# Pairing the scan groups' values in a hybrid decoder trunk on one core

## The chip, the core and the metric

The program runs on one core of a Trainium2 chip. The metric is device microseconds of one execution; the times shown are medians of several runs, and the profile is of one further execution.

## What is computed

The reference is a trunk of two layers over a sequence of 256 tokens of width 1024, float32 throughout. Each layer normalises the stream, multiplies it by one wide input matrix (1024 x 12832), and feeds three token mixers side by side: a Mamba-2 scan, sliding-window attention with sinks, and forgetting attention. Each mixer's output is gated, projected, weighted by a sigmoid gate and summed; the sum goes through one output matrix and is added to the stream. Cut to what the change touches, the scan of one group of four heads (G = 4 groups, chunks of 128 tokens, states of 128):

```python
cb = jnp.einsum('bclgn,bcsgn->bgcls', cc, bc)
y_diag = jnp.einsum('bgrcls,bcsgrp->bclgrp', cb[:, :, None] * decay, x_dt)
...
states = jnp.einsum('bcsgn,bgrcs,bcsgrp->bcgrpn', bc, decay_states, x_dt)
...
y_off = jnp.einsum('bclgn,bcgrpn,bgrcl->bclgrp', cc, prev, jnp.exp(a_cum))
return (y_diag + y_off).reshape(b, s, g, r, p)
```

## The kernel before

**Dense products.** A float32 product is made of three products of rounded halves: hi·hi, lo·hi and hi·lo. The weights come as parts of 512 KB. SyncE loads a part into a `raw` buffer (`load_part`, L363), ScalarE rounds it to `hi` (L293), VectorE subtracts to get `lo` (L294), and then the raw buffer is free. There are N_RAW = 6 raw buffers, 6 each of `hi` and `lo`, and TensorE's program holds at most AHEAD = 4 parts. A load is issued as soon as the part whose buffer it takes has been split; `load_to` (L368 on) asks for it in the order of the stream.

**Units.** Most of TensorE's row is units of 16 dense products (eight of 128x512, eight of 128x256) into one PSUM bank of the tag mm, of which there are three in a ring. The bank is emptied by ScalarE and VectorE: in `chan_sum` (L476 to L482) ScalarE copies one half (L481) and VectorE adds the other (L482); after L482 the bank can be written again, three units later. The other five banks (tag mx) serve everything else.

**What interrupts the units.** Between units the program pumps generators (`pump`, L150) that wait for a time on a model clock, for a token, or for a condition. The scan's is `ssd_group` (L855), one generator per group of heads. It loads the cumulated decays broadcast to all partitions (L861), takes a token "ssd", and then prepares: four transposes of x on TensorE, dt times x on VectorE (L871), the decay differences (L877, L885 eight times), exponentials on ScalarE, the product of dt·x with the decay to the chunk's end (L879). After a pause, one product of C and B (L897, L898) and three multiplications with the decays on VectorE (L901). Then it stands as a `Half`: a step whose products use half of the array and which should be put where other such steps stand. When it goes on, it issues the group's values: 24 matmuls of 64 columns into one mx bank (L907 to L916), and VectorE adds them to D·x (L919, twice). At the end it gives back the token.

The forgetting attention's steps are alike (`fox_quad`, L1058, and `attn_quad`, L586), one generator per quad of heads, four quads a layer: scores (16 matmuls with 64 rows into four mx banks), softmax on VectorE (L649, L658, L661) and ScalarE (L655), transposes, and then values. The values of two quads are kept back in `y.values` and issued ahead of the third quad's scores (L593 to L595); those of the last pair are issued by the last quad itself, and `y.closing` is true when only these are left. A step of TensorE that goes to half-array products and back to dense ones is called an excursion here.

**Around the scan** run the units of the gate z of the scan's branch (`u_z`, L928), whose end (`normed`, L949 to L957) needs the group's values: VectorE multiplies (L951), and splits the result for the projection (L294, L297). `u_conv`, gates (L1102) and projections follow or precede.

**What sets the order.** TensorE's row is as the program writes it. VectorE's, ScalarE's and GpSimd's rows are ordered by a scheduling layer from that program; SyncE issues loads in the stream's order. Each engine goes through its row strictly one after another.

**Tokens before.** T_SSD = 1: one group on chip at a time. Group 0, 1 and 2 go on from `Half` when another half-array step of the second branch stands ready, or at the latest 12 units of the model clock after (D_MEET); group 3 when `y.closing` is true and another stands ready:

```python
limit_ = clock["t"] + D_MEET
meets = lambda: any(m[2] == 2 and m[5] and ready(m) for m in waiting)
yield Half((lambda: y.closing and meets()) if g == 3 else lambda: clock["t"] >= limit_ or meets())
```

Of the kernel before, what the change touches and what calls it, by code (L numbers as in the profile page):

```python
# [25 lines left out]
D_K, D_Q, D_QK, D_G0, D_FOX, D_BDMA, D_BIAS, D_BC, D_SSD3 = 6.0, 5.5, 2.0, 8.0, 0.0, 4.0, 2.6, 5.5, 1.0  # L26
D_GN1, D_GN2, D_CUM, D_H, D_M = 8.0, 3.0, 17.0, (4.8, 6.4), 5.0
BUDGET = 1.35
T_PP, T_SSD, T_BIAS = 1, 1, 1
D_MEET = 12.0  # L30
D_SCAN = 18.0
D_FOLD = 8.0
N_RAW, N_SPLIT = 6, 6
AHEAD = 4
WARM = 7
FILL = 10
# [14 lines left out]
def hybrid_trunk(  # L51
# [10 lines left out]
    ps = ctx.enter_context(tc.tile_pool(name="ps", bufs=1, space=bass.MemoryType.PSUM))  # L62
    dr = ctx.enter_context(tc.tile_pool(name="dr", bufs=1, space=bass.MemoryType.DRAM))

    BUFS = dict(raw=N_RAW, hi=N_SPLIT, lo=N_SPLIT, L8=6, L16=1, L4=3, L2=8, L1=14, pp=2, qt=4,
                bias=2, st=1, sm=6)
    count = [0]

    def T(tag, shape, dtype=F32, bufs=None):
        count[0] += 1  # L70
        return sb.tile(shape, dtype, tag=tag, name=f"{tag}_{count[0]}",
                       bufs=bufs if bufs is not None else BUFS.get(tag, 1))

# [7 lines left out]
    def pmx():  # L81
        return PS("mx", 5)
# [10 lines left out]
    clock = {"t": 0.0, "n": 0}  # L93
# [9 lines left out]
    def mm(o, a, b, **kw):  # L103
        n = b.free_size()
        if a.dtype == F32R:
            clock["t"] += max(0.094, n / 2350.0)
        else:
            clock["t"] += max(0.2, n / 587.0) * (0.5 if a.free_size() == 64 or a.shape[0] == 32 else 1.0)
        nc.tensor.matmul(o, a, b, **kw)  # L109

    def transpose(o, a, i):
        clock["t"] += 0.109
        nc.tensor.transpose(o, a, i)  # L113
# [22 lines left out]
    def ready(m):  # L136
        return m[0] <= clock["t"] and allowed(m)
# [82 lines left out]
    def bc(ap, axis, n):  # L220
        s = list(ap.shape)
        s.insert(axis, n)
        return ap.unsqueeze(axis).to_broadcast(s)
# [204 lines left out]
    for l in range(L):  # L428
        y = Layer()
# [156 lines left out]
    def attn_quad(y, last, products, biases, nsink, v, vcols, sz, gated, scored=lambda: None, window=False):  # L586
# [56 lines left out]
        for p in () if window else range(2):  # L643
# [15 lines left out]
            for i in range(2):  # L659
                for b, sl in blocks:  # L660
                    ts(pp[:, i, sl], pp[:, i, sl], rs[:, 2 * i + b:2 * i + b + 1], 0.5,  # L661
                       op0=ALU.mult, op1=ALU.mult)
        yield D_FOLD if window else D_SOFT
        scored()
# [152 lines left out]
    def u_conv(y, u, c):  # L817
        def f(w):
            if u == 8:
                y.bcT = T("L8", [P, 8, S])  # L820
            if u == 0:
                y.xs = T("L8", [P, 8, S])
            dst = y.xs[:, u, :] if u < 8 else y.bcT[:, u - 8, :]
            x_ = T("L1", [P, S])
            dma_sum(y, w, c, x_)

            def taps():
                a = T("L1", [P, S])
                act(a, x_, AF.Identity, scale=y.vec[:, 48 + u:49 + u], bias=y.vec[:, 64 + u:65 + u])  # L829
                for j in (2, 1, 0):  # L830
                    s = 3 - j
                    stt(a[:, s:S], x_[:, 0:S - s], y.vec[:, 16 * j + u:16 * j + u + 1], a[:, s:S],  # L832
                        op0=ALU.mult, op1=ALU.add)
                ends_later.append(lambda: end(a))

            def end(a):
                th = T("L1", [P, S])
                act(th, a, AF.Tanh)  # L838
                stt(dst, th, 1.0, a, op0=ALU.add, op1=ALU.mult)
                if u < 8 and u % 2 == 1:  # L840
                    launch(0, ssd_group(y, u // 2), D_G0)
            after_evictions(3, taps)
            pump()
        return f
# [10 lines left out]
    def ssd_group(y, g):  # L855
        yield lambda: not any(m[2] == 1 for m in waiting)
        if g == 0:
            yield D_SCAN
        yield "bcg"
        bcg = T("L4", [P, 4, S])  # L860
        nc.scalar.dma_start(bcg, y.cumd[1, 4 * g:4 * g + 4, :].partition_broadcast(P))  # L861
        yield D_BC
        yield "ssd"
        xdt = T("L2", [P, 2, 256])
        hs = slice(4 * g, 4 * g + 4)
        p = pmx()
        for t in range(2):
            for j in range(2):
                n = 2 * t + j
                transpose(p[:, n * P:(n + 1) * P], y.xs[:, 2 * g + j, t * P:(t + 1) * P], ident)  # L870
        own = tt(xdt.rearrange("p t (h d) -> p t h d", h=4), p.rearrange("p (t h d) -> p t h d", t=2, h=4),  # L871
                 bc(y.dt[:, :, hs], 3, 64), op=ALU.mult)
        xds = T("L1", [P, 256])
        decs = []
        with tc.issue_after(own.ins):
            ds = T("ds", [P, 4], bufs=2)
            tt(ds, bcg[:, :, P - 1], y.acum[:, 0, hs], op=ALU.subtract)  # L877
            act(ds, ds, AF.Exp)
            tt(xds.rearrange("p (h d) -> p h d", h=4), xdt[:, 0, :].rearrange("p (h d) -> p h d", h=4),  # L879
               bc(ds, 2, 64), op=ALU.mult)  # L880
            for c in range(2):
                tk = slice(c * P, (c + 1) * P)
                dec = T("L2", [P, 4, P])
                for h in range(4):
                    stt(dec[:, h, :], bcg[:, h, tk], y.acum[:, c, 4 * g + h:4 * g + h + 1], negtri,  # L885
                        op0=ALU.subtract, op1=ALU.add)
                grown = act(dec, dec, AF.Exp)
                decs.append(dec)

        cross = T("L2", [P, 4, P])  # L890
        with tc.issue_after(grown.ins):
            act(cross, bcg[:, :, P:S], AF.Exp)
        decs.append(cross)
        yield D_SSD
        tokens["bcg"] += 1

        p = pmx()  # L897
        mm(p[:, 0:S], y.bcT[:, g, 0:P], y.bcT[:, 4 + g, :], start=True, stop=True)  # L898
        mm(p[:, S:3 * P], y.bcT[:, g, P:S], y.bcT[:, 4 + g, P:S], start=True, stop=True)
        for dec, c in zip(decs, (0, 2, 1)):  # L900
            tt(dec, dec, bc(p[:, c * P:(c + 1) * P], 1, 4), op=ALU.mult)  # L901
        yield D_SSD2
        limit_ = clock["t"] + D_MEET
        meets = lambda: any(m[2] == 2 and m[5] and ready(m) for m in waiting)
        yield Half((lambda: y.closing and meets()) if g == 3 else lambda: clock["t"] >= limit_ or meets())

        py = pmx()  # L907
        for c in range(2):
            for j in range(2):
                o = py[:, S * j + P * c:S * j + P * c + P]  # L910
                for s in range(c + 1):
                    for i in range(2):
                        h = 2 * j + i
                        hc = slice(64 * h, 64 * h + 64)
                        a, b = (xdt[:, c, hc], decs[c][:, h, :]) if s == 0 else (xds[:, hc], cross[:, h, :])
                        mm(o[64 * i:64 * i + 64, :], a, b, start=(s == 0), stop=(s == c))  # L916
        for j in range(2):
            u = 2 * g + j
            stt(y.xs[:, u, :], y.xs[:, u, :], y.dsk[:, u:u + 1], py[:, S * j:S * j + S], op0=ALU.mult, op1=ALU.add)  # L919
        y.scanned.add(g)  # L920
        if g == 3:
            for f in y.unscanned:
                f()
        yield D_SSD3
        tokens["ssd"] += 1
# [658 lines left out]
```

## Time and profile before

| what | value |
|---|---|
| median of 3 runs | 808.25 us (807.83 to 808.33) |
| profiled execution | 808.24 us |
| its span, first to last instruction | 806.5 us |
| granted TensorE clock | 0.999 |
| TensorE busy | 797.2 us (99%) |
| VectorE busy | 684.8 us (85%) |
| ScalarE busy | 533.7 us (66%) |
| GpSimd busy | 170.9 us (21%) |
| HBM read | 154.71 MB, 195 GB/s over the span |

A row of the timeline gives start and duration in us, the engine, the source line, the operation, what it writes and reads by the program's names, the shape, and how many like instructions in a row it groups; in brackets behind it, idle time just before and what ended it. `128*64` and `64*128` on a matmul are the rows and columns of the array that it uses; a dense product uses 128*128. A matmul's or an elementwise instruction's duration contains time that overlaps the next one, so costs are taken from one start to the next.

### The profile page before, as it was taken

Reading aid. Unit: us, or ns where it says so; the run is one execution under the profiler, and the core shown is the slowest. Engines: PE = TensorE matmul, PEld = TensorE weight load, DVE = VectorE, ACT = ScalarE, POOL = GpSimd, SP = SyncE. Lnnn points to the kernel's source line nnn. Section 1 sums busy time; section 2 is a strip of 40 time slices with the busy share of each in tenths; the row PEclk is TensorE's granted clock in tenths of the full one; section 3 lists DMA queues with packets and bytes.
Section 4 is the critical chain, followed back from the end, with each engine's and each line's share of the span. In section 5 each row is a group of like instructions: output and inputs, shape, how many; then the busy total and the mean of one; then the engine's idle time right before and its main releaser. Section 6 shows DMA issues by size and latency. Waiting matters only on the chain.

```text
span 806.5 us, 14832 instructions
## 1 busy us (share of the span) xinstructions
PE 797.2 (99%) x5162; PEld 711.2 (88%) x5162; DVE 684.8 (85%) x1414; ACT 533.7 (66%) x1144; POOL 170.9 (21%) x238
## 2 busy tenths in 40 slices
PE   8999999999999999999999999999999999999996
PEld 7998988888888988888998899888889989888896
DVE  6868999998899997795785799999879999969865
ACT  7776768875776785543665678687747768755452
POOL 3156213130320100033001741222212110002000
PEclk9999999999999999999999999999999999999999
DMA  9998987797665565676678987689986646576632
GB/s 313 268 266 178 248 222 195 212 295 226 161 212 172 170 192 171 220 249 210 215 245 259 235 206 225 158 217 281 267 229 184 194 147 200 157 248 210 210 109 75
DMA packets 138826, 170.43 MB, mean 211 GB/s; under 512 B 9352, under 2 KB 106464, under 8 KB 138752
## 3 DMA queue, kind: packets, MB, share of 16 engines
q1 hardware_dynamic: 114960, 140.53, 55.3%
q0 software_dynamic: 13328, 13.29, 10.3%
q10 hardware_dynamic: 10464, 15.67, 6.7%
q8 instruction: 41, 0.67, 0.3%
q14 instruction: 33, 0.27, 0.1%
HBM read 154.71 MB, written 2.16 MB: 195 GB/s over the span
## 4 chain that ended last, share of the span: by engine, by line
PE 97%; DVE 1%; DMA 1%; issue 0%; ACT 0%; SPq 0%
PE mm L109 84%; PE mx L109 10%; PE mx L113 3%; DMA raw<-in_w_in_dram 1%; DVE lo L294 0%; DVE L L1102 0%; SPq L189 0%; DVE L L1446 0%; ACT L L1450 0%; ACT hi L1459 0%; ACT L L1226 0%; DVE L L1201 0%; SPq L363 0%; DVE L L1205 0%; DVE L L288 0%
## 5 line engine op out<-in xcount | busy, mean ns | idle before, releaser
L109 PE MATMUL mm<-L,hi 128*128 128x512 f32 x1056 | 354.0, 387 | 0.7 <-DVE L L1102 0.5
L294 DVE TENSOR_TENSOR lo<-raw,hi 128x1024 fp32r<-128x1024 f32 (+1 forms) x276 | 312.4, 1151 | 43.8 <-ACT hi L293 41.1
L293 ACT ACTIVATE hi<-raw 128x1024 fp32r<-128x1024 f32 (+1 forms) x276 | 265.9, 982 | 60.3 <-PE mm L109 38.2
L109 PE MATMUL mm<-hi,L 128*128 128x512 f32 (+2 forms) x1168 | 303.4, 349 | 0.1
L109 PE MATMUL mm<-L,lo 128*128 128x256 f32 x1056 | 266.6, 273 | 0.0
L109 PEld LDWEIGHTS mm<-hi,L 128*128 128x128 f32 x1168 | 205.7, 190 | 23.1 <-issue 1.5
L109 PEld LDWEIGHTS mm<-L,hi 128*128 128x128 f32 x1056 | 194.9, 190 | 27.3 <-issue 4.9
L109 PEld LDWEIGHTS mm<-L,lo 128*128 128x128 f32 x1056 | 202.1, 191 | 5.4
L109 PE MATMUL mm<-lo,L 128*128 128x512 f32 (+2 forms) x584 | 201.6, 347 | 0.0
L109 PEld LDWEIGHTS mm<-lo,L 128*128 128x128 f32 x584 | 110.2, 190 | 11.0 <-DVE lo L294 0.3
L491 POOL DMA_DIRECT2D L<-L x68 | 60.3, 911 | 191.9 <-ACT L L490 180.2
L1071 POOL TENSOR_SCALAR_AFFINE_SELECT bias<-bias 128x128 f32<-128x128 f32 x64 | 33.4, 555 | 77.2 <-DMA bias<-cumd 77.2
L832 DVE SCALAR_TENSOR_TENSOR L<-L,vec,L 128x255 f32<-128x255 f32 (+2 forms) x96 | 46.2, 481 | 2.1 <-ACT L L829 0.3
L489 ACT ACTIVATE L<-mm 128x256 f32<-128x256 f32 x84 | 32.0, 381 | 19.5 <-PE mm L109 14.1
L655 ACT ACTIVATE pp<-pp,nm 128x128 f32<-128x128 f32 x64 | 28.2, 443 | 22.1 <-DVE nm L649 22.1
L1105 ACT ACTIVATE L<-L 128x512 f32<-128x512 f32 x24 | 15.1, 630 | 35.7 <-DVE L L1102 31.2
L491 POOL DMA_DIRECT2D qt<-L x16 | 13.8, 862 | 76.3 <-ACT qt L490 76.3
L613 ACT ACTIVATE pp<-pp,nm 128x128 f32<-128x128 f32 x32 | 12.6, 394 | 25.6 <-DVE nm L618 24.9
L1138 POOL TENSOR_TENSOR L<-L,L 128x512 f32<-128x512 f32 x8 | 12.0, 1496 | 73.9 <-DVE L L1137 73.9
L490 ACT ACTIVATE L<-mm 128x256 f32<-128x256 f32 x68 | 26.2, 386 | 1.2 <-DMA L<-L 1.2
L1102 DVE TENSOR_TENSOR L<-mm,L 128x512 f32<-128x512 f32 x22 | 15.1, 686 | 11.7 <-PE mm L109 9.1
L838 ACT ACTIVATE L<-L 128x256 f32<-128x256 f32 x32 | 13.4, 418 | 16.5 <-DVE L L832 16.4
(212 smaller groups left out, 918.3 us busy)
## 6 DMA issues: line engine op xcount, KB each, us to landing
raw<-in_w_in_dram SPq DMA_DIRECT2D x191, 512.0 KB, 5.2
raw<-in_w_proj_dram SPq DMA_DIRECT2D x48, 512.0 KB, 6.2
L<-L POOLq DMA_DIRECT2D x72, 128.0 KB, 5.4
raw<-in_w_out_dram SPq DMA_DIRECT2D x16, 512.0 KB, 4.8
bias<-cumd ACTq DMA_DIRECT2D x16, 256.0 KB, 3.2
L<-cumd ACTq DMA_DIRECT2D x8, 512.0 KB, 6.5
L<-in_gate_bias_dram ACTq DMA_DIRECT2D x12, 256.0 KB, 5.9
qt<-L POOLq DMA_DIRECT2D x16, 128.0 KB, 6.0
```

The costliest lines, as they stand in the source:

```text
L109: nc.tensor.matmul(o, a, b, **kw)
L113: nc.tensor.transpose(o, a, i)
L293: keep(act)(hi, src, AF.Copy)
L294: keep(tt)(lo, src, hi.bitcast(F32), op=ALU.subtract)
L489: act(halves(lo), ordered(p[:, S:2 * S]), AF.Copy)
L490: last = act(halves(out), ordered(p[:, 0:S]), AF.Copy)
L491: nc.gpsimd.dma_start(out, lo, accum_op=ALU.add)
L655: act(pp[:, i, sl], pp[:, i, sl], AF.Exp, scale=-1.0, bias=nm[:, e:e + 1], accum_out=sums[:, e:e + 1])
L832: stt(a[:, s:S], x_[:, 0:S - s], y.vec[:, 16 * j + u:16 * j + u + 1], a[:, s:S], op0=ALU.mult, op1=ALU.add)
L1071: nc.gpsimd.affine_select(out=bias[:, i, dst], in_=bias[:, i, src], compare_op=ALU.is_ge, fill=NEG, base=0, pattern=[[-1, P]], channel_mul ...
L1102: tt(halves(g), p, halves(y.gb), op=ALU.add)
L1105: finish(act(g, g, AF.Tanh, scale=0.5))
```

## The change

Two scan groups may be on chip at a time (T_SSD 2). Groups 0 and 1 now wait until the first pair of quads' attention values are ready to go, groups 2 and 3 until the last pair's values are all that is left; the time limit D_MEET is gone. Group 3 starts 9 units of the model clock after its token (D_APART). The pool of 2-KB buffers L2, which hold the decays and dt·x, grows from 8 to 10, and the raw weight buffers go from 6 to 5 to make room.

```diff
-T_PP, T_SSD, T_BIAS = 1, 1, 1
-D_MEET = 12.0
+T_PP, T_SSD, T_BIAS = 1, 2, 1
 D_SCAN = 18.0
+D_APART = 9.0
 D_FOLD = 8.0
-N_RAW, N_SPLIT = 6, 6
+N_RAW, N_SPLIT = 5, 6
...
-    BUFS = dict(raw=N_RAW, hi=N_SPLIT, lo=N_SPLIT, L8=6, L16=1, L4=3, L2=8, L1=14, pp=2, qt=4,
+    BUFS = dict(raw=N_RAW, hi=N_SPLIT, lo=N_SPLIT, L8=6, L16=1, L4=3, L2=10, L1=14, pp=2, qt=4,
                 bias=2, st=1, sm=6)
...
         yield D_BC
         yield "ssd"
+        if g == 3:
+            yield D_APART
         xdt = T("L2", [P, 2, 256])
...
         yield D_SSD2
-        limit_ = clock["t"] + D_MEET
         meets = lambda: any(m[2] == 2 and m[5] and ready(m) for m in waiting)
-        yield Half((lambda: y.closing and meets()) if g == 3 else lambda: clock["t"] >= limit_ or meets())
+        with_values = (lambda: y.values and y.values[0] is not None) if g < 2 else lambda: y.closing
+        yield Half(lambda: with_values() and meets())
```

Behind L863 the line numbers of the changed kernel are 2 higher (L871 becomes L873, L885 becomes L887, L901 becomes L903, L919 becomes L921, L940 becomes L942, L951 becomes L953).

**On TensorE**, in layer 0. Before, at the first excursion, the values of group 0 (bank mx_2765) stand directly ahead of the scores of quad 0 (reading `qt`), behind the last product of a unit:

```order
L109 MATMUL mm_2712<-L_73_376,hi_2640 128x512
L109 MATMUL mx_2765<-L_517_2522,L_513_2510 64x128 x4
L109 MATMUL mx_2765<-L_518_2528,L_513_2510 64x128 x2
L109 MATMUL mx_2765<-L_519_2534,L_515_2517 64x128 x2
L109 MATMUL mx_2765<-L_518_2528,L_513_2510 64x128 x2
L109 MATMUL mx_2765<-L_519_2534,L_515_2517 64x128 x2
L109 MATMUL mx_2784<-qt_2165 128x128
L109 MATMUL mx_2785<-qt_2165 128x128
L109 MATMUL mx_2784<-qt_2165 128x256
L109 MATMUL mx_2785<-qt_2165 128x256
```

After, groups 0 and 1 (mx_3356 and mx_3371) stand ahead of the attention values of quads 0 and 1 (mx_3386 and, behind this piece, mm_3395) and the scores of quad 2, at what is the third excursion:

```order
L109 MATMUL mx_3356<-L_517_2526,L_512_2508 64x128 x2
L109 MATMUL mx_3356<-L_518_2532,L_514_2515 64x128 x2
L109 MATMUL mx_3356<-L_517_2526,L_512_2508 64x128 x2
L109 MATMUL mx_3356<-L_518_2532,L_514_2515 64x128 x2
L109 MATMUL mx_3371<-L_531_2599,L_527_2587 64x128 x4
L109 MATMUL mx_3371<-L_532_2605,L_527_2587 64x128 x2
L109 MATMUL mx_3371<-L_533_2611,L_529_2594 64x128 x2
L109 MATMUL mx_3371<-L_532_2605,L_527_2587 64x128 x2
L109 MATMUL mx_3371<-L_533_2611,L_529_2594 64x128 x2
L109 MATMUL mx_3386<-L_600_2937,L_62_328 64x256 x2
L109 MATMUL mx_3386<-L_600_2937,L_62_328 64x128 x2
```

Group 0 and group 1 have moved behind by two excursions and one; the scores of quads 0 and 1 are left alone in the first and second. Group 2, which stood here before, has moved to the fifth excursion, where group 3 was and is.

**On VectorE**, in layer 0. Before, group 2's preparation stands ahead of the third excursion, behind quad 1's softmax (L661):

```order
L661 TENSOR_SCALAR pp_3086<-pp_3086,rsum_3123 128x256
L871 TENSOR_TENSOR L_638_3160<-mx_3161,dt_1481 128x512
L482 TENSOR_TENSOR qt_2995<-mm_3129,qt_2995 128x256
L877 TENSOR_TENSOR ds_3168<-L_536_2620,acum_1745 128x4
L885 TENSOR_SCALAR L_642_3172<-L_536_2620,acum_1745,negtri_79 128x128 x4
L879 TENSOR_TENSOR L_640_3167<-L_638_3160,ds_3168 128x256
L885 TENSOR_SCALAR L_643_3178<-L_536_2620,acum_1745,negtri_79 128x128 x4
L294 TENSOR_TENSOR lo_3218<-raw_2922,hi_3217 128x1024
L482 TENSOR_TENSOR L_589_2886<-mm_3186,L_589_2886 128x256
L294 TENSOR_TENSOR lo_3232<-raw_2936,hi_3231 128x1024
L940 TENSOR_SCALAR L_589_2886<-L_646_3205,L_589_2886 128x256
L482 TENSOR_TENSOR L_589_2886<-mm_3208,L_589_2886 128x256
```

After, group 2's multiplications by the C·B product (L903, bank mx_3602), and then the whole preparation of group 3, stand between quad 2's softmax and quad 3's, behind the third excursion; group 2's own L873 to L887 stand some 15 rows ahead of this piece, directly behind quad 2's softmax:

```order
L482 TENSOR_TENSOR L_718_3582<-mm_3583,L_718_3582 128x256
L903 TENSOR_TENSOR L_698_3496<-L_698_3496,mx_3602 128x512
L903 TENSOR_TENSOR L_699_3502<-L_699_3502,mx_3602 128x512
L903 TENSOR_TENSOR L_700_3508<-L_700_3508,mx_3602 128x512
L873 TENSOR_TENSOR L_723_3618<-mx_3619,dt_1479 128x512
L879 TENSOR_TENSOR ds_3626<-L_606_2966,acum_1743 128x4
L887 TENSOR_SCALAR L_727_3630<-L_606_2966,acum_1743,negtri_79 128x128 x2
L881 TENSOR_TENSOR L_725_3625<-L_723_3618,ds_3626 128x256
L887 TENSOR_SCALAR L_727_3630<-L_606_2966,acum_1743,negtri_79 128x128 x2
L887 TENSOR_SCALAR L_728_3636<-L_606_2966,acum_1743,negtri_79 128x128 x4
L942 TENSOR_SCALAR L_718_3582<-L_738_3675,L_718_3582 128x256
L482 TENSOR_TENSOR L_730_3644<-mm_3645,L_730_3644 128x256
```

One group's preparation has moved from the stretch ahead of the third excursion into the stretch behind it, which now holds two.

## The prediction, made before the changed kernel was run

> **What bounds the kernel now.** I read the page first (busy time, then the chain that ended last), then the waits of TensorE and of SyncE's queue, then the stretch of layer 0 that the change touches, row by row. From the page:
>
> ```profile
> PE 797.2 (99%) x5162; PEld 711.2 (88%) x5162; DVE 684.8 (85%) x1414; ACT 533.7 (66%) x1144; POOL 170.9 (21%) x238
> ...
> PE 97%; DVE 1%; DMA 1%; issue 0%; ACT 0%; SPq 0%
> ```
>
> TensorE is the bound from end to end. What it waits for in the whole program is this, in total, times and longest:
>
> ```profile
> PE mx L113 <- POOL ident masks.py:199: 1.5, 1, 1.5
> PE mx L109 <- ACT hi L1459: 0.6, 2, 0.3
> PE mm L109 <- DVE L L1102: 0.5, 1, 0.5
> ```
>
> That is 2.6 us. So no wait is left inside a layer that the change could remove. It can only gain by making TensorE's own row of products shorter, and it loses wherever another engine comes too late. Busy time by stretches around the third excursion to half-array products (PE, PEld, DVE, ACT, POOL with instructions, then clock, DMA share, GB/s):
>
> ```profile
> 249.00:257.00 8.00, 8.00 (x87) 6.64 (x84) 6.39 (x26) 3.03 (x14) 0.00 (x0) 1.00 0.47 142
> 257.00:273.00 16.00, 16.00 (x107) 14.66 (x107) 15.62 (x35) 12.69 (x27) 4.17 (x8) 1.00 0.52 165
> 273.00:294.00 21.00, 21.00 (x140) 18.91 (x138) 19.82 (x56) 18.17 (x48) 0.00 (x0) 1.00 0.58 176
> ```
>
> From 257 to 294 us VectorE is busy for 35.4 of 37 us, 96%: behind this excursion there is hardly room on it. It must also empty the three mm banks in turn, and this is how near it comes to holding TensorE up there, in layer 0 and in layer 1:
>
> ```profile
> 280.85 0.41 DVE L482 TENSOR_TENSOR L<-mm,L 128x256 f32<-128x256 f32 x1
> ...
> 282.61 0.46 PE L109 MATMUL mm<-L,hi 128*128 128x512 f32 x1
> ...
> 675.94 0.42 DVE L482 TENSOR_TENSOR L<-mm,L 128x256 f32<-128x256 f32 x1
> ...
> 677.65 0.46 PE L109 MATMUL mm<-L,hi 128*128 128x512 f32 x1
> ```
>
> Each L482 reads the bank that the product below it writes again. The read ends at 281.26 and the product starts at 282.61: 1.35 us to spare; in layer 1, 676.36 and 677.65: 1.29 us. These are the smallest margins of the mm banks in either layer.
>
> **What TensorE gains.** The rows of the first and third excursion:
>
> ```profile
> 206.07 1.53 PE L109 MATMUL mx<-L,L 128*64 128x128 f32 x24
> 207.53 1.58 PE L109 MATMUL mx<-qt 64*128 64x128 f32 x16
> ...
> 248.66 2.83 PE L109 MATMUL mx<-L,L 128*64 128x128 f32 x40
> 251.32 1.47 PE L109 MATMUL mm<-L,L 128*64 128x256 f32 x16
> 252.72 1.58 PE L109 MATMUL mx<-qt 64*128 64x128 f32 x16
> 254.23 0.48 PE L109 MATMUL mm<-L,hi 128*128 128x512 f32 x1
> ...
> 256.96 0.60 PE L113 MATMUL mx<-ident,L 128*128 128x128 f32 x4
> 257.31 0.46 PE L109 MATMUL mm<-L,hi 128*128 128x512 f32 x1
> ...
> 265.91 0.82 PE L109 MATMUL mx<-L 128*128 128x256 f32 x4
> 266.57 0.82 PE L113 MATMUL mx<-ident,pp 128*128 128x128 f32 x6
> ```
>
> From start to start, 24 matmuls of a scan group's values take 1.46 us ahead of scores, the 16 of one half of the attention values 1.40 ahead of scores, and one quad's scores 1.51. The 40 at 248.66 are such a 24 and the other half's 16 without a change of form between them or behind them: 2.66 us, 0.20 less than 1.46 + 1.40. So a change of form (128\*64 to 64\*128) costs about 0.10 us, and values that stay among their own form take 1.36 per group. A group's transposes of x take 0.35, its product of C and B with the step to the next kind 0.66. The unit of 16 dense products behind the excursion lasts 254.23 to 256.96, 2.73 us, where units without an excursion ahead take 2.62, again 0.1.
>
> So what counts is changes of form, in, between and out. In the order, groups 0 and 1 went out with the scores of quads 0 and 1 before, group 2 with the first attention values and the scores of quad 2, group 3 with the last values, and quad 3's scores went alone: 3 + 3 + 3 + 2 + 2 = 13 changes per layer. After: scores 0 alone, scores 1 alone, groups 0 and 1 with values and scores 2, scores 3 alone, groups 2 and 3 with the last values: 2 + 2 + 3 + 2 + 2 = 11. The number of excursions is five in both: the pairing replaces a sharing that was there, with scores in place of values. Two changes a layer at 0.10 us are −0.4 in the program. Transposes and C·B products leave the dense stream 13 times before and after; three steps a layer from a C·B product to transposes become one, at some 0.05 to 0.09 us each −0.2. TensorE gains **−0.6 us**.
>
> The Trainium skill, "TensorEngine Tiling (Array Packing)", section "Key Properties", says that a change of tiling mode drains TensorE. By that rule, changes are counted as here, and the rows above agree with 0.10 us; if only the way out of and back into dense products were paid, the sum below would be 0.4 us higher.
>
> **What VectorE has to do later.** The order shows group 2's preparation (before at 235 to 247 us, ahead of the third excursion) behind it. Its price, and the rows around it:
>
> ```profile
> 258.92 0.68 DVE L871 TENSOR_TENSOR L<-mx,dt 128x512 f32<-128x512 f32 x1
> 259.52 0.41 DVE L482 TENSOR_TENSOR qt<-mm,qt 128x256 f32<-128x256 f32 x1
> 259.85 0.15 DVE L877 TENSOR_TENSOR ds<-L,acum 128x4 f32<-128x4 f32 x1
> 259.92 1.13 DVE L885 SCALAR_TENSOR_TENSOR L<-L,acum,negtri 128x128 f32<-128x128 f32 x4
> 260.97 0.42 DVE L879 TENSOR_TENSOR L<-L,ds 128x256 f32<-128x256 f32 x1
> ...
> 262.49 1.21 DVE L294 TENSOR_TENSOR lo<-raw,hi 128x1024 fp32r<-128x1024 f32 x1
> 263.62 0.41 DVE L482 TENSOR_TENSOR L<-mm,L 128x256 f32<-128x256 f32 x1
> ...
> 276.48 0.18 DVE L658 RECIPROCAL rsum<-sums 128x4 f32<-128x4 f32 x1 [0.27 <-ACT pp L655]
> ...
> 278.24 0.18 DVE L658 RECIPROCAL rsum<-sums 128x4 f32<-128x4 f32 x1 [0.34 <-ACT pp L655]
> ...
> 281.18 0.41 DVE L951 TENSOR_TENSOR L<-L,L 128x256 f32<-128x256 f32 x1
> 281.51 1.22 DVE L294 TENSOR_TENSOR lo<-raw,hi 128x1024 fp32r<-128x1024 f32 x1
> 282.65 0.48 DVE L297 SCALAR_TENSOR_TENSOR L<-L,vec,L 128x256 fp32r<-128x256 f32 x1
> 283.05 0.42 DVE L940 SCALAR_TENSOR_TENSOR L<-L,L 128x256 f32<-128x256 f32 x1
> ```
>
> From start to start: L871 0.60, L482 0.33, L877 0.07, L885 0.265 each, L879 0.33, one `lo` (L294) 1.13, L951 0.33, L297 0.40.
>
> The eviction to watch is that of the sixth unit behind the third excursion; the ninth unit writes its bank again (before, the seventh and the tenth). I count from the excursion's start, T = 248.66 before.
>
> - **VectorE.** Before, L871 starts at T + 10.26 and the read of L482 ends at T + 32.60. After, the softmax of quad 2 starts 1.36 later, since one more group's values go ahead of its scores: L871 at T + 11.62. From there to the watched L482 the order after has, beyond what stood there before, one L871, one L877, eight L885, one L879, two L951 and one L297: 0.60 + 0.07 + 2.12 + 0.33 + 0.66 + 0.40 = 4.18; and one `lo` and one L482 fewer, −1.46. So 2.72 more. Two short waits for ScalarE's exponentials, 0.27 and 0.34 us in this softmax block before, are covered now by other rows that the order puts there: −0.6. The read ends at T + 32.60 + 1.36 + 2.72 − 0.6 = T + 36.1. Adding up the order's rows one by one, by the durations above, gives T + 35.7. I take 35.9.
> - **TensorE.** Before it comes to the reused bank at T + 33.95. After, one unit fewer lies ahead (−2.62), 1.36 more of scan values, a C·B product of its own (0.66), and the transposes of the other group (0.35): T + 33.7.
>
> TensorE waits 35.9 − 33.7 = **2.2 us**, once per layer; layer 1 has the same margin and the same order, so **4.4 us**. Bounds: nothing if VectorE finds 2.2 us that I don't see; 3 us a layer if nothing of its short waits is covered. Behind the wait everything on TensorE's row stands (it is one queue), and VectorE has caught up by it, so that the next two evictions, some 2.1 and 2.6 us apart by the same rows, keep pace with units of 2.62.
>
> **What five raw buffers cost.** A load goes into the buffer that `lo` has left, now that of the part five back instead of six:
>
> ```profile
> SPq L363 <- DVE lo L294: 422.7, 176, 13.5
> ...
> raw<-in_w_in_dram SPq DMA_DIRECT2D x191, 512.0 KB, 5.2
> ...
> 23.84 1.06 ACT L293 ACTIVATE hi<-raw 128x1024 fp32r<-128x1024 f32 x1 [0.57 <-DMA raw<-in_w_in_dram]
> ...
> 28.47 2.35 DVE L294 TENSOR_TENSOR lo<-raw,hi 128x1024 fp32r<-128x1024 f32 x2
> ...
> 29.74 0.48 PE L109 MATMUL mm<-lo,L 128*128 128x512 f32 x1
> ```
>
> The 422.7 us are waiting of SyncE's queue alone: loads stand ready early, and a later start costs only where the landing then comes after its use. In the bulk of a layer a part is used 6 to 20 us after the buffer five back is free, against 5.2 us from issue to landing. Two places are tight. At the start the tenth part's `hi` waited for its load (0.57 us), and the ninth part's `lo` ended just ahead of the product at 29.74; loads would start up to 2 us later, with the DMA queues full until about 20 us, so that a later start is first only another place in the queue: **+0.3**, bounds 0 and 1.9. At the turn of the layers one load starts some 8 us later and lands about when its `hi` is due: **+0.3**, bounds 0 and 1.
>
> **The sum.** The profiled execution took 808.24 us (span 806.5), the median of the runs is 808.25, so no correction: 808.24 − 0.6 + 4.4 + 0.3 + 0.3 = **812.6 us**.
>
> **The rivals.**
>
> - *Nothing late (not slower).* VectorE idles 8.00 − 6.39 = 1.6 us from 249 to 257 us. If the rows moved behind the excursion's start fall into that, so that L871 comes sooner, and the added rows run 0.6 us shorter than counted, the read ends at T + 33.7 and nothing waits. It decides there: earlier than T + 33.7 the change is worth −0.6 plus what the loads cost, **807.6 to 809.2, about 808.2**. Against it: those waits are for TensorE's values and scores, which come in their own time, and from there on the stretch is 96% busy.
> - *Raw buffers or a second late bank (slower still).* The start-up's 1.9 and the turn's 1.0 in full, or a further wait of about 1 us a layer at the gate's bank or the group norm: 812.6 + 2 to 5 = **814.6 to 817.6**.
> - *The pairing saves excursions, faster.* Had each of the four groups had an excursion of its own (two changes, 0.2 us), pairing them with values would save three or four a layer, up to 1.6 us, **806.6**, with no engine late. The rows at 206.07 and 248.66 show groups sharing an excursion before. This is also the rival that the change doesn't do what it says: the pairs do come about in the order, but replace a sharing that was there.
>
> **How the numbers follow.** VectorE late in both layers (1 to 3 us each, 809.9 to 815): 0.62. Nothing late: 0.22. Still slower: 0.12. Faster: 0.04. The predicted time is that of the first, 812.6. The range takes in its bounds and most of the second case: 807.9 to 815.2. A measurement here can tell about 0.2%, 1.6 us, from no change: 806.6 to 809.9 is "same". Of the first case nothing lies inside it; of the second nearly all does. So slower 0.75, same 0.20, faster 0.05.
>
> **What would show it.** In the profile after: a wait of TensorE for L482 (mm bank) of about 2.2 us some 34 us behind the third excursion's start, in both layers; VectorE near 100% in the 25 us ahead of it; five half-array excursions per layer; the first 30 us within 0.5 us of before. I am wrong if TensorE's waits stay at 2.6 us (VectorE reaches T + 33.7 in time), if a wait for `hi` or `lo` stands among the largest (raw buffers), or if the products themselves take less time than the 0.6 us less that I count.

## The result, and the profile after

The changed kernel takes **815.03 us** (median of 5 runs, 814.19 to 816.33) against 807.85 us before (807.47 to 808.33): ratio 1.0089, 95% interval 1.0077 to 1.0100, 7.2 us slower. The profiled execution took 815.03 us, its span is 813.3 us, 6.8 more than before. One execution of the run with four L4 buffers below took 1037.74 us at a granted clock of 0.753, and that run's figures leave it out.

The same two lines of the page of the changed kernel, busy time and the chain that ended last:

```profile
PE 797.5 (98%) x5162; PEld 710.9 (87%) x5162; DVE 685.3 (84%) x1414; ACT 535.2 (66%) x1144; POOL 168.4 (21%) x238
...
PE 83%; DVE 11%; ACT 2%; DMA 2%; issue 1%; SPq 0%; ACTq 0%; DVEq 0%
```

TensorE is busy for as long as before, within 0.3 us, but the chain now leaves it: VectorE has 11% of it, before 1%. No engine has over 1.5 us more to do; it is done at the wrong moment. TensorE's waits name the moments (total us, times, longest):

```profile
PE mm L109 <- DVE L L482: 3.5, 2, 1.8
PE mx L113 <- POOL ident masks.py:199: 1.5, 1, 1.5
PE mm L109 <- DVE lo L294: 1.5, 1, 1.5
PE mm L109 <- ACT L L695: 0.9, 2, 0.5
PE mx L109 <- ACT hi L1461: 0.8, 2, 0.5
PE mm L109 <- DVE L L1104: 0.6, 2, 0.3
PE mx L113 <- DVE sums L639: 0.3, 1, 0.3
```

Four are new: L482 twice, `lo` once, L695 twice, and a short one for L639. To see what each is worth I take the start of the same dense product (counted through the program) in both traces:

| product | before | after | later by |
|---|---|---|---|
| the `lo` product near 30 us, in the start-up | 29.74 | 31.17 | 1.43 |
| ahead of layer 0's scan | 151.88 | 153.37 | 1.49 |
| behind layer 0's scan | 309.21 | 313.15 | 3.94 |
| ahead of layer 1's scan | 546.93 | 551.16 | 4.24 |
| behind layer 1's scan | 704.26 | 710.91 | 6.66 |

So 1.4 us are lost in the start-up, 2.45 and 2.4 in the two scans, 0.3 in between.

**The eviction.** VectorE and TensorE of the changed kernel in layer 0, at the places that the prediction names (T, the third excursion's start, is now 251.38):

```profile
263.68 0.68 DVE L873 TENSOR_TENSOR L<-mx,dt 128x512 f32<-128x512 f32 x1
...
275.74 0.68 DVE L873 TENSOR_TENSOR L<-mx,dt 128x512 f32<-128x512 f32 x1
...
287.38 0.41 DVE L482 TENSOR_TENSOR L<-mm,L 128x256 f32<-128x256 f32 x1
```

```profile
285.35 0.82 PE L113 MATMUL mx<-ident,pp 128*128 128x128 f32 x6
287.94 0.45 PE L109 MATMUL mm<-L,hi 128*128 128x512 f32 x1 [1.77 <-DVE L L482]
```

Two preparations (two L873) now lie in this stretch. The read of L482 ends at 287.38 + 0.41 = 287.79, T + 36.4. The six transposes take 0.57 us where nothing waits (before, 282.03 to 282.61), so the product could have started at 285.92; it started at 287.94, 2.02 us late. Busy time of the stretch (PE, PEld, DVE, ACT, POOL):

```profile
259.00:288.00 29.00, 27.23 (x181) 24.61 (x179) 28.36 (x96) 24.41 (x66) 5.09 (x8) 1.00 0.42 124
```

VectorE is busy for 28.36 of 29 us, 98%.

**The third excursion** itself, TensorE and then ScalarE:

```profile
251.38 4.14 PE L109 MATMUL mx<-L,L 128*64 128x128 f32 x64
255.98 1.58 PE L109 MATMUL mm<-L,L 128*64 128x256 f32 x16 [0.46 <-ACT L L695]
257.49 1.58 PE L109 MATMUL mx<-qt 64*128 64x128 f32 x16
259.00 0.48 PE L109 MATMUL mm<-L,hi 128*128 128x512 f32 x1
```

```profile
252.36 0.42 ACT L941 ACTIVATE L<-L 128x256 f32<-128x256 f32 x1 [0.49 <-DVE L L482]
255.33 1.09 ACT L695 ACTIVATE L<-mx 128x512 f32<-128x512 f32 x2 [2.56 <-PE mx L109]
```

The excursion takes 7.62 us to the next dense product; before it took 5.57, and two groups in place of one should add 1.36, so 0.69 are lost. ScalarE stands idle for 2.56 us ahead of two copies of transposed probabilities (L695), released by TensorE itself, at the moment when the first half of the attention values is through. In the code the copies of a quad go to a buffer of the pool L4, which has three. The decays that a group loads (L861) are in the same pool. Groups 2 and 3 have theirs loaded by then and cannot use them before groups 0 and 1 have given back their tokens, which they now do in this very excursion. That leaves one L4 buffer for two quads.

**The start-up.** ScalarE, VectorE and TensorE of the changed kernel:

```profile
25.27 1.06 ACT L293 ACTIVATE hi<-raw 128x1024 fp32r<-128x1024 f32 x1 [2.37 <-DMA raw<-in_w_in_dram]
25.32 0.37 ACTq L1100 DMA_DIRECT2D L<-in_gate_bias_dram  x1
26.23 1.66 ACT L293 ACTIVATE L<-L 128x512 fp32r<-128x512 f32 x3
```

```profile
26.88 0.69 DVE L294 TENSOR_TENSOR L<-L,L 128x512 fp32r<-128x512 f32 x1 [2.05 <-ACT L L293]
...
29.89 4.76 DVE L294 TENSOR_TENSOR lo<-raw,hi 128x1024 fp32r<-128x1024 f32 x6
```

```profile
31.17 0.48 PE L109 MATMUL mm<-lo,L 128*128 128x512 f32 x1 [1.48 <-DVE lo L294]
```

The tenth part's `hi` starts at 25.27 instead of 23.84, since its load came later. Its own first product is some 6 us away. But behind it on ScalarE stand the halves of the normalised stream (26.23), VectorE waits for these (2.05 us), and only behind them comes the ninth part's `lo` (29.89), whose data had been there for long. TensorE waits for that.

The Trainium skill, "TensorE: Matmul & The Clock Gate", section "Architectural detail: the array is 16× 32×32, not 1× 128×128", says that ScalarE and VectorE take their instructions strictly in order. The rows agree: the copies at 26.23 stand behind a `hi` that they do not need.

### The profile page after: what moved, and what is told of

The parts are those of the page before. It is cut to its first block, busy times and chain, and to the rows that moved or that the text cites. A ratio compares the mean times of both kernels' runs of the same rounds, so it can differ in the third digit from the quotient of the medians.

```text
span 813.3 us, 14833 instructions
## 1 busy us (share of the span) xinstructions
PE 797.5 (98%) x5162; PEld 710.9 (87%) x5162; DVE 685.3 (84%) x1414; ACT 535.2 (66%) x1144; POOL 168.4 (21%) x238
## 4 chain that ended last, share of the span: by engine, by line
PE 83%; DVE 11%; ACT 2%; DMA 2%; issue 1%; SPq 0%; ACTq 0%; DVEq 0%
PE mm L109 72%; PE mx L109 8%; DVE lo L294 3%; PE mx L113 3%; DMA raw<-in_w_in_dram 2%; DVE L L887 1%; ACT pp L655 1%; DVE L L832 1%; DVE pp L661 1%; DVE L L903 0%; DVE L L482 0%; DVE L L942 0%; DVE pp L649 0%; ACT pp L613 0%; ACT hi L293 0%
## 5 line engine op out<-in xcount | busy, mean ns | idle before, releaser
L490 ACT ACTIVATE L<-mm 128x256 f32<-128x256 f32 x68 | 26.2, 386 | 1.2 <-DMA L<-L 1.2
L984 POOL TENSOR_TENSOR sm<-sm,mhalf 128x8 f32<-128x8 f32 x2 | 3.4, 1686 | 101.0 <-DVE sm L982 101.0
```

What stands on the lines that cost most here:

```text
L490: last = act(halves(out), ordered(p[:, 0:S]), AF.Copy)
```

## The experiments

Beside each ran the kernel before, with medians of 807.97 to 807.99 us. The theory (A): three losses that add up, VectorE's second preparation behind the third excursion, the shortage of L4 buffers, and the fifth raw buffer's loss at the start. Rivals stand with each run.

### Five raw buffers alone

The kernel before, with

```diff
-N_RAW, N_SPLIT = 6, 6
+N_RAW, N_SPLIT = 5, 6
```

> The kernel before with five raw buffers instead of six and nothing else. Theory A (the start-up loss of the changed kernel belongs to the raw buffers): TensorE waits about 1.5 us for lo (L294) near 30 us, and the time is 809.2 to 809.8, 1.4 to 2.0 us over before. Rival (the start-up loss comes from the moved order): no such wait, 807.5 to 808.4.

Measured: 810.74 us, ratio 1.0035 (1.0022 to 1.0047), 2.8 us over before; the profiled span is 2.1 us longer. TensorE's waits contain

```profile
PE mm L109 <- DVE lo L294: 1.1, 1, 1.1
PE mx L113 <- DMA L<-in_x_dram: 0.4, 1, 0.4
PE mx L113 <- DVE pp L642: 0.3, 1, 0.3
PE mx L113 <- DVE sums L639: 0.3, 1, 0.3
```

and the same `lo` product starts at 31.22 with a wait of 1.15 us. The start-up loss belongs to the raw buffers, not to the order. The time is 0.9 us above the range that I expected: two short waits in the window attention (L642, L639), which the kernel before does not have, come on top.

### Four L4 buffers

The changed kernel, with

```diff
-    BUFS = dict(raw=N_RAW, hi=N_SPLIT, lo=N_SPLIT, L8=6, L16=1, L4=3, L2=10, L1=14, pp=2, qt=4,
+    BUFS = dict(raw=N_RAW, hi=N_SPLIT, lo=N_SPLIT, L8=6, L16=1, L4=4, L2=8, L1=14, pp=2, qt=4,
```

> The changed kernel with four L4 buffers instead of three, paid by eight L2 buffers instead of ten. Theory A (in the third excursion the copies of quad 1's transposed probabilities wait for an L4 buffer that the values of quad 0 still read): TensorE's wait for ScalarE's L695 of about 0.5 us per layer goes, the third excursion takes 6.9 us from its start to the next dense product instead of 7.6, and the time falls by 1.0 to 1.5 us to 813.5 to 814; the wait for L482 stays at 1.8 us per layer. Rival (ScalarE is late by its own work, or L2 is what is short): the wait stays or grows, 815 or more.

Measured: 818.89 us, ratio 1.0136 (1.0119 to 1.0153). The place did what was expected:

```profile
253.67 4.14 PE L109 MATMUL mx<-L,L 128*64 128x128 f32 x64
257.64 1.47 PE L109 MATMUL mm<-L,L 128*64 128x256 f32 x16
259.04 1.58 PE L109 MATMUL mx<-qt 64*128 64x128 f32 x16
260.55 0.48 PE L109 MATMUL mm<-L,hi 128*128 128x512 f32 x1
```

6.88 us from start to the next dense product, no wait for L695 left; the 64 matmuls take 3.97. But the time rose by 4 us, against my number. The waits:

```profile
PE mm L109 <- DVE lo L294: 4.0, 3, 1.4
PE mm L109 <- DVE L L482: 3.5, 2, 1.8
```

Two more waits for `lo` came up, 1.3 us at 195.09 and 1.4 at 594.64, ahead of the first excursion of each layer. This run also has two L2 buffers fewer. So the cause of the wait for L695 is shown, but not that a fourth buffer would pay.

### Four L4 buffers with ten L2 buffers

The changed kernel, with

```diff
-    BUFS = dict(raw=N_RAW, hi=N_SPLIT, lo=N_SPLIT, L8=6, L16=1, L4=3, L2=10, L1=14, pp=2, qt=4,
+    BUFS = dict(raw=N_RAW, hi=N_SPLIT, lo=N_SPLIT, L8=6, L16=1, L4=4, L2=10, L1=11, pp=2, qt=4,
```

> The changed kernel with four L4 buffers and ten L2 buffers, paid by eleven L1 buffers. Theory A (the run with eight L2 buffers lost its 4 us to the two L2 buffers taken, by waits for lo and a longer last excursion): the third excursion takes 6.9 us, no wait for L695, a single wait for lo (start-up), and the time falls by 1 to 1.5 us to 813.5 to 814. Rival (the fourth L4 buffer itself lets loads start that delay the parts): lo waits as there, 816 or more.

Measured: 818.60 us, ratio 1.0134 (1.0120 to 1.0147). Again no wait for L695, and the third excursion takes 6.88 us in both layers, 0.74 less than in the changed kernel. But ahead of layer 0's first excursion 4.1 us more had gathered than in the changed kernel, among them waits for L642 (1.3 us), L490 (1.2) and `lo` (0.8). The expected total failed twice. The wait for L490 is the price of the L1 buffers (see the run with eleven of them in the kernel before); what of the rest belongs to the fourth L4 buffer and what to the order of VectorE's and ScalarE's rows, which comes out otherwise with other pools, stays open.

### Group 2 early

The changed kernel, with

```diff
-with_values = (lambda: y.values and y.values[0] is not None) if g < 2 else lambda: y.closing
+with_values = (lambda: True) if g < 2 else lambda: y.closing
```

> The changed kernel, except that groups 0 and 1 may go on as soon as another half-array step is ready (with the first scores) and do not wait for the attention values. Group 2's preparation then stands ahead of the third excursion again. Theory A (what makes L482 late is that preparation behind the third excursion): TensorE's waits for L482 and for L695 are gone in both layers, the time falls by 4.5 to 6 us to 809 to 810.5, and what is left over before is the raw buffers' 1.6 us. Rival (VectorE is late there because the softmax comes later, or because of group 3 alone): a wait for L482 of over 1 us stays, 812 or more.

Measured: 811.40 us, ratio 1.0046 (1.0031 to 1.0061), 3.6 us less than the changed kernel. All of TensorE's waits in it:

```profile
PE mx L113 <- POOL ident masks.py:199: 1.5, 1, 1.5
PE mm L109 <- DVE lo L294: 1.2, 1, 1.2
PE mx L113 <- DVE pp L642: 0.8, 1, 0.8
PE mx L113 <- DMA L<-in_x_dram: 0.4, 1, 0.4
PE mx L109 <- DVE L L903: 0.4, 2, 0.2
PE mx L113 <- DVE sums L639: 0.3, 1, 0.3
```

L482 and L695 are gone in both layers. The gain is smaller than the 4.5 that I gave as the least. Against five raw buffers alone each scan is 0.6 us longer, and part of it stands at mx banks, for instance the scores behind the C·B product that now stands directly ahead of them (L903).

### Group 3 later

The changed kernel, with

```diff
-D_APART = 9.0
+D_APART = 20.0
```

> The changed kernel with group 3 held back by 20 instead of 9 units of the model clock; its preparation then stands behind quad 3's softmax on VectorE, while group 2's stays behind the third excursion. Theory A (two preparations in the stretch ahead of the sixth unit's L482 are what makes it late, by their length alone): the wait for L482 is gone, the wait for L695 stays, and the time falls by 3 to 4 us to 811 to 812, unless the last values or the group norm then come late and give some of it back. Rival (not the preparation's length but the later softmax): the wait for L482 stays over 1 us, 814 or more.

Measured: 821.11 us, ratio 1.0164 (1.0148 to 1.0180). The wait for L482 is gone and the one for L695 stays, as expected, but the time rose by 6 us, where I expected 3 to 4 us less unless the group norm came late. It did. The two longest of TensorE's waits, and the place of the first in layer 0:

```profile
PE mx L109 <- DVE L L959: 6.4, 2, 3.2
PE mm L109 <- DVE lo L294: 1.9, 1, 1.9
```

```profile
310.94 0.63 PE L109 MATMUL mx<-L,ones 128*32 128x256 f32 x6
314.78 1.06 PE L109 MATMUL mx<-L,ones 128*32 128x256 f32 x2 [3.21 <-DVE L L959]
```

Group 3's preparation, moved behind quad 3's softmax, frees the mm bank and makes the sums for the group norm late: 3.2 us a layer instead of 1.8. With both preparations behind the third excursion VectorE has too much to do before the group norm; in these two versions, where it stands decides which product pays.

The longer wait also cost more than itself. The granted TensorE clock (the third number from the end) right behind it, in layer 0:

```profile
314.00:316.00 2.00, 1.22 (x3) 0.42 (x4) 2.00 (x4) 1.46 (x3) 0.00 (x0) 0.62 0.51 133
316.00:318.00 2.00, 2.00 (x6) 1.61 (x7) 2.00 (x3) 0.78 (x2) 0.00 (x0) 0.53 0.74 244
318.00:320.00 2.00, 2.00 (x11) 1.76 (x10) 2.00 (x4) 0.00 (x0) 0.00 (x0) 1.00 0.81 192
```

The trace has the clock at 0.5 for 3.41 us from 314.46, and again from 717.24 in layer 1; the changed kernel's shows no such fall behind its waits of 1.8 us. The eight dense products from 315.77 take 2.85 us, the same eight in the changed kernel (from 313.15) 1.83. With the two sums ahead of them, that is some 1.9 us a layer on top of the wait, an estimate from these rows: about half of the 8 us by which the two profiled executions differ.

### Six raw buffers in the changed kernel

The changed kernel, with

```diff
-N_RAW, N_SPLIT = 5, 6
+N_RAW, N_SPLIT = 6, 6
...
-    BUFS = dict(raw=N_RAW, hi=N_SPLIT, lo=N_SPLIT, L8=6, L16=1, L4=3, L2=10, L1=14, pp=2, qt=4,
+    BUFS = dict(raw=N_RAW, hi=N_SPLIT, lo=N_SPLIT, L8=6, L16=1, L4=3, L2=10, L1=11, pp=2, qt=4,
```

> The changed kernel with six raw buffers, paid by eleven L1 buffers of 1 KB instead of fourteen; TensorE's, VectorE's and ScalarE's rows stand as in the changed kernel. Theory A (raw buffers and VectorE's lateness add up): the wait for lo near 30 us is gone and the time falls by what five buffers cost alone, 2 to 2.8 us, to 812.2 to 813; the waits for L482 and L695 stay. Rival (the start-up's loss hides part of the rest, so that it is given back later): 814 or more.

Measured: 813.95 us, ratio 1.0073 (1.0059 to 1.0087), 1.1 us less. The `lo` product starts at 29.21 without a wait; L482 and L695 stay with 1.8 and 0.5 us a layer. The gain is smaller than the 2 us that I gave as the least, since a new wait stands at 76 us:

```profile
76.52 0.48 PE L109 MATMUL mm<-L,hi 128*128 128x512 f32 x1 [0.96 <-ACT L L490]
```

### Eleven L1 buffers in the kernel before

The kernel before, with

```diff
-    BUFS = dict(raw=N_RAW, hi=N_SPLIT, lo=N_SPLIT, L8=6, L16=1, L4=3, L2=8, L1=14, pp=2, qt=4,
+    BUFS = dict(raw=N_RAW, hi=N_SPLIT, lo=N_SPLIT, L8=6, L16=1, L4=3, L2=8, L1=11, pp=2, qt=4,
```

> The kernel before with eleven L1 buffers instead of fourteen and nothing else: the price that the runs with six raw buffers paid. Theory A (the wait of 1.0 us for L490 near 76 us in the changed kernel with six raw buffers belongs to the L1 buffers): 808.8 to 809.3, about 1 us over before. Rival (that wait belongs to the changed order): 807.6 to 808.4.

Measured: 808.91 us, ratio 1.0010 (1.0001 to 1.0020), 0.9 us over before, with a new wait for L490 of 0.7 us among TensorE's, and 1.5 us for L1102, before 0.5. The price of the L1 buffers is about that, so six raw buffers are worth some 2 us in the changed kernel (1.1 + 0.9), in line with the 2.1 between the spans of the first run (2.8 between its medians).

### Group 2 early with six raw buffers, two ways to pay

To the edit that prepares group 2 early, the first adds

```diff
-N_RAW, N_SPLIT = 5, 6
+N_RAW, N_SPLIT = 6, 6
...
-    BUFS = dict(raw=N_RAW, hi=N_SPLIT, lo=N_SPLIT, L8=6, L16=1, L4=3, L2=10, L1=14, pp=2, qt=4,
+    BUFS = dict(raw=N_RAW, hi=N_SPLIT, lo=N_SPLIT, L8=6, L16=1, L4=3, L2=10, L1=11, pp=2, qt=4,
```

and the second pays with another pool:

```diff
-N_RAW, N_SPLIT = 5, 6
+N_RAW, N_SPLIT = 6, 6
...
-    BUFS = dict(raw=N_RAW, hi=N_SPLIT, lo=N_SPLIT, L8=6, L16=1, L4=3, L2=10, L1=14, pp=2, qt=4,
+    BUFS = dict(raw=N_RAW, hi=N_SPLIT, lo=N_SPLIT, L8=6, L16=1, L4=3, L2=9, L1=13, pp=2, qt=4,
```

> The kernel in which groups 0 and 1 go with the first scores and group 2's preparation stands early, now with six raw buffers (eleven L1 buffers pay). Theory A (only the raw buffers and some short waits for PSUM banks in the scan were left): 2.1 to 2.8 us less than with five, 808.6 to 809.3, within 0.2% of before and not faster, since 0.6 us per layer of short waits stand against 0.2 us saved. Rival (without the raw loss the saved changes of form show): 807.4 or less.

> The kernel with groups 0 and 1 at the first scores, group 2 prepared early and six raw buffers, now with nine L2 and thirteen L1 buffers: the version that the runs so far point to. Theory A (what it lost with eleven L1 buffers was in part those): 808.4 to 809.6, within about 0.2% of before, since some 0.5 us of short waits per layer in the scan stay. Rival (it loses by its order alone): 810 or more.

Measured: the first 810.62 us, ratio 1.0032 (1.0020 to 1.0044), 1.3 us above the range that I gave; the second 808.88 us, ratio 1.0011 (1.0002 to 1.0020). In the second all of TensorE's waits but the one of the start add up to 1.0 us:

```profile
PE mm L109 <- DVE L L1104: 0.6, 2, 0.4
PE mx L113 <- DVE sums L639: 0.2, 1, 0.2
PE mx L113 <- DMA L<-in_x_dram: 0.2, 1, 0.2
```

This keeps the changed kernel's pairs (groups 0 and 1 together, now at the first scores, 2 and 3 together) and takes away most of its three losses: 6.2 us faster than the changed kernel, and no faster than before. In its third excursion ScalarE stands idle ahead of a copy of L695 once more:

```profile
250.40 0.60 ACT L695 ACTIVATE L<-mx 128x512 f32<-128x512 f32 x1 [1.22 <-PE mx L109]
```

In both layers that excursion takes 4.52 us, where 5.57 − 1.36 = 4.21 would do with one group fewer than before, and the first takes 4.53, where 2.97 + 1.36 = 4.33 would do with one more. So 0.5 us a layer are still lost there, though the list of waits has none of it, and each scan is 0.25 us longer than before. What it would take without them, no run shows. No version faster than before came up.

## Why the prediction was right, and where its sizes were off

**The time itself** lies just under the upper end of the range, 815.2, and 2.4 us above the predicted 812.6. That the range holds it is in part luck. By the prediction's own cases it falls into the second rival, 814.6 to 817.6 with a chance of 0.12, and not into the first case, which ended at 815. That rival came about in part: 1.4 of its 1.9 us at the start, and a further wait of 0.7 us a layer, though neither at the gate's bank nor at the group norm. Of the signs, the wait for L482 in both layers, the full VectorE and the five excursions came; two went against the prediction: the first 30 us are not within 0.5 us of before, and a wait for `lo` stands among the largest. The main term stood; what follows takes the terms one by one.

**TensorE alone decides, and has next to nothing to win:** right. Its busy time is the same within 0.3 us, and the best version ends 0.1% above before. The scan's 2.45 us in layer 0 are 2.02 (L482) + 0.69 (L695) − 0.26, and the last, a remainder, fits the −0.3 a layer counted in advance. Of these, the changes of form can be read directly: layer 0's five excursions take 17.08 us before and 17.60 after, 16.91 without the 0.69, so 0.17 less, forecast 0.2. The Trainium skill's rule on changes of form ("TensorEngine Tiling (Array Packing)", "Key Properties") is borne out: with four L4 buffers 64 matmuls take 3.97 us, where pieces that each end in a change of form would take 1.46 + 1.46 + 1.40 = 4.32.

**VectorE late at the sixth unit's eviction:** right in place and cause, and near in size: 2.02 us, forecast 2.2. From L873 to the end of the read VectorE took 24.1 us, forecast 24.3 (35.9 − 11.6). The excursion ahead was 0.7 us longer, which delays both sides: the read ended at T + 36.4, forecast 35.9, and TensorE could have come at T + 34.5, forecast 33.7. So the two errors largely cancel, and of the 2.02 us 0.15 lie between the end of the read and the product's start, which the forecast did not count; to that extent the closeness is luck. Group 2 early and group 3 later each took the wait away.

**The start-up:** the step "a later start is first only another place in the queue: +0.3, bounds 0 and 1.9" was mis-sized; it cost 1.43, inside its bounds. The row that I quoted showed a `hi` that already waited 0.57 us for its load, and I did not look at what stands behind it on ScalarE, by which it had to be weighed. What had slack in its use had none in its place. The turn of the layers, also +0.3, cost nothing that the traces show (3.94 behind the first scan; the 0.3 more at 4.24 stands ahead of the second, with a wait for L1104 of 0.3).

**The copies of quad 1 (L695):** not in the prediction at all, 0.69 us a layer. I looked at the raw buffers, which the change resizes, and at PSUM, not at a pool that it leaves alone but holds for longer. That the pool was short is shown by two runs in which a fourth buffer removed the wait; which tiles held the other two is read from the code alone.

The terms forecast add up to 4.4 us. Measured, they are 1.4 (start-up), 4.0 (L482), 1.4 (L695) and −0.5 (products), 6.3 together; with 0.3 at L1104 and 0.2 in small pieces they make the 6.8 between the spans (7.2 between the medians).

## What to carry to other kernels

When an edit moves work on an engine that is nearly full, add up its rows between two points at which the bounding engine needs it, before and after; that gave 2.2 us against 2.0 measured. Moving group 3's rows further behind only changed who waits; moving group 2's ahead took the wait away. A buffer pool is not only what the edit resizes: ask for every pool which tiles stay alive longer now. And a prefetch that comes late costs what stands behind its first reader in that engine's row, however far off its own use is.

## What was not expected of the hardware

The fall of the granted clock to 0.5 behind the two waits of 3.2 us, and not behind those of 1.8, was not foreseen in the run with group 3 later. New too is how dear small pools are: three of fourteen 1-KB buffers cost 0.9 us and one of six raw buffers 2.8 us. A fourth 4-KB buffer removed a loss of 0.7 us in each layer; with the buffers that paid for it, the time still rose by 4 us.
